# Gate, shift and scale of the first layer's modulation: native fp32 products on TensorE in four column groups, in place of sums on VectorE

## The chip, the cores and the metric

The kernel runs on one core of a Trainium2 chip, in one launch. The metric is device time in microseconds (us). Before the change it takes 1473.36 us, the median of 3 runs that lie between 1472.47 and 1473.88. Engines are named as the profile names them: PE is TensorE, DVE is VectorE, ACT is ScalarE, POOL is GpSimd, and SP is SyncE, which issues the transfers from DRAM.

## What is computed

Two transformer blocks on 256 tokens of 1024 channels. The first block has two layers, each an attention and an MLP; the second has four parallel branches and a mixture of experts. Six vectors of 1024 numbers per layer, the modulation, shift, scale and gate the data of that layer. The part of the reference that matters here is the first layer:

```python
cond = silu(c)                                   # [1, 1024]
mod = cond @ ada_w[layer] + ada_b[layer]         # [1, 6 * 1024], float32
sh1, sc1, g1, sh2, sc2, g2 = split(mod, 6)
h = rms_norm(x, norm_mix) * (1 + sc1) + sh1
x = x + g1 * even_mixer(h, ...)                  # latent and dilated attention
h = rms_norm(x, norm_mlp) * (1 + sc2) + sh2
x = x + g2 * relu(h @ w1) ** 2 @ w2
```

The change concerns `g1`, `sh2` and `sc2` of the first layer: 3072 columns of `ada_w[0]`, a product of one row of 1024 with a matrix of 1024 x 3072 (12.6 MB in float32). They are not needed before the attention's output projection is added to `x`.

## The kernel before

Tokens lie in two tiles of 128 partitions. Weights come from DRAM in units of up to 128 x 1024 floats (`unit`, `load`), each into one of four buffers named `raw`. ACT copies a unit into `hi` at reduced precision (line 318), DVE subtracts to get the rest `lo` (line 319), and in this layer POOL does every fourth subtraction instead. A product is then three PE passes over the two parts (`mm3`, lines 330 to 332) into the PSUM tiles `pj`, `ps` or `po`. Operands that are not split (attention's queries, keys, values and transposes) are multiplied as native fp32.

Layer one, `even`, runs in this order:

1. `first_columns`: the modulation's first 16 blocks of 128 columns (`sh1`, `sc1`), the normed input, and 672 columns of the projection.
2. The two latents (`latent`), normed and transposed (line 382); then two chunks of the values of the dilated heads (`dv`), two chunks of latent queries (`uq`), two of latent keys and values (`ukv`). After each chunk `fill` puts a few tiles of the modulation between (`FILL_FIRST`).
3. `weave`: the latent attention of 8 heads (`causal`, lines 635, 637, 1014), and after each head one step of the projection of the dilated queries and keys (`dilated_qk`: four chunks of four units each; `qk`, lines 552 to 606, norms and rotates them on ACT, POOL and DVE), and some tiles of the modulation (`FILL_EVEN`).
4. `dilated`: the attention of the dilated heads (lines 956 and 974), woven with the output projection and more tiles (`FILL_DIL`).
5. The rows for gate and norm are spread over the partitions (`row`, line 452), `x` is updated and normed, and the MLP starts.

A tile of the modulation is 128 columns of `ada_w`, transposed on the host, 128 x 1024: SP loads it (line 417) into one of two buffers named `ada`, and one DVE instruction (line 432, in the profile `CUSTOM_DVE_ANT_0 ada<-ada,crow`) multiplies it with the row `crow` that every partition holds and sums along the row; a short second instruction reads the sum out. Blocks 16 to 39 of 128 columns are 24 such tiles.

SP's queue is one list for all transfers. An entry waits until its buffer is free, and everything behind it waits too. What order the instructions of an engine get is made by a scheduling layer from the order in which the program writes them; `fill` asks that its tiles come on DVE behind the last subtraction. Each engine then runs its list in order.

## Time and profile before

| | |
|---|---|
| median of 3 runs | 1473.36 us |
| the profiled execution, first to last instruction | 1489.5 us |
| PE busy in it | 1376.8 us (92%) |
| DVE busy in it | 1171.3 us (79%) |
| ACT busy in it | 841.3 us (56%) |
| mean granted TensorE clock | 0.952 of full speed |
| DVE tiles of the modulation in the whole program | 132, 167.9 us |
| layer one's attention part (from the latents to the norm of the MLP) | about 52 us to 240 us |

The profiled execution is 16 us, or 1.1%, longer than the median of the runs, as profiling adds to it; steps are read from it and a result is scaled by 1473.36 / 1489.5 = 0.989. A busy PE is not a PE at its peak: the granted clock stands beside each stretch, 1.00 for 2.4 GHz and 0.50 for 1.2 GHz. A native fp32 product stands in the trace as two records of PE.

### The profile page before, as it was taken

What the parts mean: (1) busy time and instruction counts of PE and PEld (TensorE: products, weight loads), DVE (VectorE), ACT (ScalarE), POOL (GpSimd) and SP (SyncE); (2) the same over time, 40 slices, a digit from 0 to 9 for tenths busy, and PEclk for the clock granted to TensorE, in tenths of its full rate; (3) what the DMA queues carried; (4) which work ended last, traced back from release to release, by engine and by line L of the source; (5) the groups of instructions that cost most, each with busy time, mean ns of one, the idle gap of its engine ahead of it and who ended that gap; (6) DMA issues with size and microseconds to landing.
All of it is one profiled execution on the core that took longest, in us unless ns stands there. A gap on an engine that the chain in (4) does not pass through costs nothing.

```text
span 1489.5 us, 20624 instructions
## 1 busy us (share of the span) xinstructions
PE 1376.8 (92%) x7338; PEld 1140.7 (77%) x7338; DVE 1171.3 (79%) x1923; ACT 841.3 (56%) x1334; POOL 210.2 (14%) x217
## 2 busy tenths in 40 slices
PE   5778899999998989999999999999997799999996
PEld 4657678989876657988989797677785688888884
DVE  8878776787786856798775679997675898888896
ACT  4355565355544554545665556555545487777764
POOL 5557601000033301000014000000002000000001
PEclk9789899999989969999999999999999899999998
DMA  9556554889855323878744667444552599999994
GB/s 360 168 185 222 198 170 156 305 312 339 317 182 163 118 75 102 290 247 294 254 128 127 225 227 229 144 144 154 179 186 89 187 358 342 324 326 325 320 340 148
DMA packets 94414, 333.55 MB, mean 224 GB/s; under 512 B 10720, under 2 KB 11872, under 8 KB 94304
## 3 DMA queue, kind: packets, MB, share of 16 engines
q1 hardware_dynamic: 94304, 332.17, 65.5%
q8 instruction: 59, 0.97, 0.3%
q14 instruction: 51, 0.42, 0.1%
HBM read 331.08 MB, written 1.05 MB: 223 GB/s over the span
## 4 chain that ended last, share of the span: by engine, by line
PE 54%; DVE 17%; DMA 14%; issue 5%; ACT 4%; POOL 4%; SPq 0%; DVEq 0%; ACTq 0%; POOLq 0%
PE pj L330 6%; DMA raw<-in_w_dram 6%; PE pj L331 6%; PE pj L332 6%; DMA ada<-in_adaT_dram 5%; PE ps L330 5%; PE ps L332 5%; PE ps L331 5%; DVE lo L319 4%; PE ps L382 3%; DVE ada L432 3%; ACT hi L318 2%; POOL hr L471 2%; DMA raw<-in_gu_dram 2%; PE po L330 1%
## 5 line engine op out<-in xcount | busy, mean ns | idle before, releaser
L318 ACT CAST hi<-raw 128x1024 fp32r<-128x1024 f32 (+3 forms) x331 | 333.1, 1017 | 223.7 <-DMA raw<-in_w_dram 80.2
L319 DVE TENSOR_TENSOR lo<-raw,hi 128x1024 fp32r<-128x1024 f32 (+1 forms) x313 | 378.8, 1221 | 96.7 <-ACT hi L318 94.4
L432 DVE CUSTOM_DVE_ANT_0 ada<-ada,crow 128x1024 f32<-128x1024 f32 x132 | 167.9, 1280 | 32.0 <-DMA ada<-in_adaT_dram 32.0
L330 PE MATMUL pj<-hi,H 128*128 128x512 f32 (+3 forms) x392 | 154.9, 396 | 11.4 <-ACT H L734 9.0
L332 PE MATMUL pj<-hi,H 128*128 128x512 f32 (+3 forms) x392 | 151.9, 388 | 5.5 <-POOL H L737 3.4
L331 PE MATMUL pj<-lo,H 128*128 128x512 f32 (+3 forms) x392 | 151.7, 388 | 3.0 <-DVE lo L319 2.9
L1116 PE MATMUL ps<-H,lo 128*128 128x256 f32 x408 | 116.0, 284 | 2.8 <-DVE lo L319 2.7
L330 PE MATMUL pj<-hi,A 128*128 128x512 f32 (+1 forms) x293 | 115.9, 396 | 2.8 <-DVE w L879 2.0
L331 PE MATMUL pj<-lo,A 128*128 128x512 f32 (+1 forms) x293 | 115.6, 394 | 1.7 <-DVE lo L319 1.6
L1114 PE MATMUL ps<-H,hi 128*128 128x256 f32 x408 | 115.9, 284 | 0.0
L1115 PE MATMUL ps<-H,hi 128*128 128x256 f32 x408 | 115.4, 283 | 0.0
L332 PE MATMUL pj<-hi,A 128*128 128x512 f32 (+1 forms) x293 | 114.5, 391 | 0.0
L330 PEld LDWEIGHTS pj<-hi,H 128*128 128x128 f32 x392 | 76.9, 196 | 33.6 <-ACT H L734 11.6
L332 PEld LDWEIGHTS pj<-hi,H 128*128 128x128 f32 x392 | 77.3, 197 | 21.1 <-POOL H L737 6.2
L331 PEld LDWEIGHTS pj<-lo,H 128*128 128x128 f32 x392 | 77.9, 199 | 14.7 <-DVE lo L319 3.8
L1116 PEld LDWEIGHTS ps<-H,lo 128*128 128x128 f32 x408 | 78.2, 192 | 3.8 <-DVE lo L319 3.8
L1114 PEld LDWEIGHTS ps<-H,hi 128*128 128x128 f32 x408 | 78.2, 192 | 0.6 <-DVE w L543 0.2
L1115 PEld LDWEIGHTS ps<-H,hi 128*128 128x128 f32 x408 | 78.2, 192 | 0.4
L330 PE MATMUL ps<-hi,A 128*128 128x512 f32 x180 | 71.2, 396 | 0.0
L332 PE MATMUL ps<-hi,A 128*128 128x512 f32 x180 | 70.3, 391 | 0.0
L331 PE MATMUL ps<-lo,A 128*128 128x512 f32 x180 | 70.3, 390 | 0.0
L330 PEld LDWEIGHTS pj<-hi,A 128*128 128x128 f32 x293 | 55.6, 190 | 17.2 <-issue 4.4
(544 smaller groups left out, 3300.3 us busy)
## 6 DMA issues: line engine op xcount, KB each, us to landing
ada<-in_adaT_dram SPq DMA_DIRECT2D x132, 512.0 KB, 4.8
raw<-in_w_dram SPq DMA_DIRECT2D x128, 512.0 KB, 5.5
raw<-in_gu_dram SPq DMA_DIRECT2D x78, 512.0 KB, 5.9
raw<-in_in_dram SPq DMA_DIRECT2D x60, 512.0 KB, 4.6
raw<-in_down_dram SPq DMA_DIRECT2D x37, 512.0 KB, 5.6
crow<-in_gu_dram SPq DMA_DIRECT2D x34, 512.0 KB, 5.9
raw<-in_odd_in_dram SPq DMA_DIRECT2D x24, 512.0 KB, 4.8
raw<-in_even_in_dram SPq DMA_DIRECT2D x24, 384.0 KB, 3.7
```

The source lines that it names most:

```text
L318: self.nc.scalar.copy(hi, src)
L319: end = (engine or self.nc.vector).tensor_tensor(lo, src, hi, ALU.subtract)
L330: mm(ps, ah, bh, start=start, stop=False)
L331: mm(ps, ah, bl, start=False, stop=False)
L332: mm(ps, al, bh, start=False, stop=stop)
L382: self.nc.tensor.transpose(out, in_, self.ident[:p, :p])
L432: nc.vector.tensor_tensor_reduce(out=o, in0=wt, in1=r, scale=1.0, scalar=0.0, op0=ALU.mult, op1=ALU.add, accum_out=m[:, j:j + 1])
L471: nc.gpsimd.tensor_tensor(out, ss, self.mhalf[:, :ss.shape[1]], ALU.pow)
L1114: mm(ps[:, n % 2], wh, hh[:, k], start=k == 0 and n % 2 == 0, stop=False)
L1115: mm(ps[:, n % 2], wh, hl[:, k], start=False, stop=False)
L1116: mm(ps[:, n % 2], wl, hh[:, k], start=False, stop=k == 7 and n % 2 == 1)
```

## The change

The 24 DVE tiles of blocks 16 to 39 go. In their place stand three sums, one for each vector (gate, shift, scale), each of four steps. A step takes 2 x 128 rows of `ada_w[0]` and 1024 of its columns, 1 MB, laid out on the host in this order (`adaN`). Four native fp32 matmuls work on it: the column `ccol` of silu(c), repeated 32 times, is the stationary operand, 512 columns of weights the moving one, and each matmul has its own group of 32 of the array's columns, so its own 32 partitions of one PSUM tile `po`. After four steps ACT copies the sum out (`pe_end`), four small matmuls with a selection matrix turn it into columns and add the two halves of the rows, and DVE adds the bias.

The steps are no longer called by `fill` but by `steps`: 2, 2, 1, 1, 1, 1 after the six chunks of stage 2, and one after every second step of `dilated_qk`. The first eight steps are loaded into the large places `O0` and `O1` in turn, which stage 1 no longer needs and attention's output takes later; the last four into the two `ada` buffers. A step's load is issued two steps ahead of its use, once its place has been read. The stage `dilated` has none left.

```diff
+EVEN_ROOMS = ["O0", "O1"] * 4 + ["ada"] * 4
+EVEN_AHEAD = 2
+PE_EVEN = 0
-FILL_FIRST = [3, 3, 0, 0, 0, 1]
-FILL_DIL = [0, 2, 3, 0]
+FILL_FIRST = [2, 2, 1, 1, 1, 1]
-FILL_EVEN = [4, 2, 1, 2, 0, 0, 3, 2]
+FILL_EVEN = [0, 1, 0, 1, 0, 1, 0, 1]
+PE_COLS = [(512, (2048, 2560)), (512, (3072, 3584)), (512, (4096, 4608))]
...
+    def steps(self, g, n):
+        for _ in range(n):
+            next(g, None)
+
+    def with_steps(self, main, g, ns):
+        ns = iter(ns)
+        for _ in main:
+            self.steps(g, next(ns, 0))
+            yield
+        self.steps(g, 99)
...
+    def pe_load(self, parts, w):
+        n = 2 * len(parts) * w
+        for t in parts:
+            ap = bass.AP(tensor=self.A["adaN"].tensor, offset=self.pe_off, ap=[[4 * w, P], [1, t.shape[1]]])
+            self.nc.sync.dma_start(t, ap)
+            self.pe_off += t.shape[1]
+        self.pe_off += 4 * w * (P - 1)
+
+    def pe_part(self, acc, s, parts, w):
+        nc = self.nc
+        for kk in range(2):
+            t = parts[0][:, kk * 2 * w:] if len(parts) == 1 else parts[kk]
+            c = self.ccol[:, 2 * s + kk:2 * s + kk + 1].to_broadcast([P, 32])
+            for i in range(2):
+                r0 = 64 * i + 32 * kk
+                nc.tensor.matmul(acc[r0:r0 + 32, :w], c, t[:, i * w:i * w + w], start=s == 0, stop=s == 3)
+
+    def pe_even(self, at):
+        def load(s):
+            if s < len(EVEN_ROOMS):
+                r = EVEN_ROOMS[s]
+                parts = [self.T([P, D], "ada") for _ in range(2)] if r == "ada" else [self.slot(r, [P, 2 * D])]
+                self.pe_load(parts, 512)
+                tiles.append(parts)
+        tiles = []
+        for s in range(EVEN_AHEAD):
+            load(s)
+        yield
+        for s in range(len(EVEN_ROOMS)):
+            if s % 4 == 0:
+                sums = self.ps(tag="po")
+            self.pe_part(sums, s % 4, tiles[s], 512)
+            load(s + EVEN_AHEAD)
+            if s % 4 == 3:
+                j = PE_COLS[at + s // 4][1][0] // P
+                m = self.mod[0][:, j:j + 8]
+                self.nc.vector.tensor_tensor(m.rearrange("p (i j) -> p i j", i=2), self.pe_end(sums, 512),
+                                             self.cols[:, j:j + 8].rearrange("p (i j) -> p i j", i=2), ALU.add)
+            yield
+
+    def pe_end(self, acc, w):
+        nc = self.nc
+        rows = self.w()
+        nc.scalar.copy(rows[:, :w], acc[:, :w])
+        n = w // P
+        ps = self.ps()
+        for j in range(n):
+            nc.tensor.matmul(ps[:, j:j + n + 1:n], rows[:, j * P:j * P + P], self.sel, start=True, stop=True)
+        return ps[:, :2 * n].rearrange("p (i j) -> p i j", i=2)
...
-        for a, b in ((16, 24), (24, 40)):
-            self.later(0, [self.crow0], [mod], range(a, b), pool=POOL_EVEN)
+        gemv = self.pe_even(PE_EVEN)
+        next(gemv)
...
-            self.fill(FILL_FIRST[c])
+            self.steps(gemv, FILL_FIRST[c])
...
-                   dilated_qk(), FILL_EVEN, PACE_MLA)
+                   self.with_steps(dilated_qk(), gemv, FILL_EVEN), (), PACE_MLA)
...
-        self.weave(self.after_tail(dilated()), out, FILL_DIL, PACE_DIL)
+        self.weave(self.after_tail(dilated()), out, (), PACE_DIL)
```

The selection matrix adds two columns to the constants. Everything behind `dilated` is unchanged. In the order that the program gives the engines the change shows at three places; names carry buffer numbers, and line numbers of the changed kernel are its own.

SP's list at the second chunk of `dv` and the start of `uq`, before (`raw` are weights to split, `ada` tiles of the modulation):

```order
L305 DMA raw_623<-in_even_in_dram 128x768
L305 DMA raw_629<-in_even_in_dram 128x768
L417 DMA ada_620<-in_adaT_dram 128x1024
L305 DMA raw_635<-in_even_in_dram 128x768
L305 DMA raw_641<-in_even_in_dram 128x768
L417 DMA ada_699<-in_adaT_dram 128x1024
L417 DMA ada_702<-in_adaT_dram 128x1024
L305 DMA raw_708<-in_uq_dram 128x768
```

The same place after the change:

```order
L732 DMA O_139_623<-in_adaN_dram 128x2048
L732 DMA O_140_629<-in_adaN_dram 128x2048
L312 DMA raw_631<-in_even_in_dram 128x768
L312 DMA raw_637<-in_even_in_dram 128x768
L312 DMA raw_643<-in_even_in_dram 128x768
L312 DMA raw_649<-in_even_in_dram 128x768
L732 DMA O_155_711<-in_adaN_dram 128x2048
L732 DMA O_156_717<-in_adaN_dram 128x2048
L312 DMA raw_727<-in_uq_dram 128x768
```

Two loads of 1 MB now stand ahead of the four units of a chunk, where single tiles of half a MB stood between them.

PE's list between `first_columns` and the first chunk of `dv`, before (`ps` from `w` are the latents' transposes):

```order
L382 MATMUL ps_472<-consts_67,w_470 128x128 x3
L382 MATMUL ps_494<-consts_67,w_484 128x128 x2
L330 MATMUL pj_562<-hi_540,H_31_145 128x384
L330 MATMUL pj_563<-hi_540,H_31_145 128x384
L331 MATMUL pj_562<-lo_541,H_31_145 128x384
```

The same place after:

```order
L401 MATMUL ps_472<-consts_67,w_470 128x128 x3
L401 MATMUL ps_494<-consts_67,w_484 128x128 x2
L744 MATMUL po_618<-O_120_536,ccol_65 32x512
L401 MATMUL ps_507<-consts_67,w_505 128x128 x3
L401 MATMUL ps_529<-consts_67,w_519 128x128 x2
L744 MATMUL po_618<-O_120_536,ccol_65 32x512 x3
L744 MATMUL po_618<-O_121_538,ccol_65 32x512 x4
L337 MATMUL pj_566<-hi_544,H_31_145 128x384
```

The first two steps, eight matmuls, and the transposes of the second tile of tokens moved ahead of the first chunk's products. Steps three and four stand in the same way between the two chunks of `dv`, five and six between `dv` and `uq`, and the others among later work.

DVE's list in the weave, around the third and fourth chunk of `dilated_qk`, before:

```order
L319 TENSOR_TENSOR lo_1495<-raw_1492,hi_1494 128x768
L1025 RECIPROCAL sm_1461<-sm_1461 128x2
L606 TENSOR_TENSOR w_1385<-w_1385,hr_1394 128x384
L623 TENSOR_SCALAR sc_1463<-sc_1463,sm_1461 128x128
L432 ISA ada_1555,mod_1_61<-ada_1555,crow_75 128x1024
L432 ISA mod_1_61 128x1
L432 ISA ada_1558,mod_1_61<-ada_1558,crow_75 128x1024
L432 ISA mod_1_61 128x1
L606 TENSOR_TENSOR w_1435<-w_1435,hr_1444 128x384
```

The like place after:

```order
L625 TENSOR_TENSOR w_1477<-w_1477,hr_1486 128x384
L1101 RECIPROCAL sm_1507<-sm_1507 128x2
L642 TENSOR_SCALAR sc_1509<-sc_1509,sm_1507 128x128
L326 TENSOR_TENSOR lo_1936<-raw_1933,hi_1935 128x1024
L593 TENSOR_TENSOR w_1588<-pj_1544,tabk_1350 128x384
```

The tiles of line 432 that stood between attention's and the projection's short instructions are gone, and nothing takes their place on DVE but one addition of 128 x 8 for each of the three sums.

## Rows read from the trace of the kernel before

**Rows 1.** Busy time by stretch: length, PE, PEld, DVE, ACT, POOL; clock, DMA share, GB/s.

```profile
63.00:84.00 21.00, 19.66 (x109) 18.38 (x107) 16.88 (x30) 8.71 (x18) 7.08 (x6) 1.00 0.72 238
84.00:108.00 24.00, 16.39 (x73) 12.05 (x74) 17.84 (x42) 14.06 (x33) 20.04 (x30) 0.85 0.45 154
108.00:150.00 42.00, 35.98 (x188) 32.91 (x187) 37.19 (x79) 21.71 (x51) 26.96 (x24) 0.91 0.68 219
150.00:180.00 30.00, 25.00 (x127) 20.79 (x126) 25.24 (x49) 17.25 (x39) 24.83 (x22) 0.90 0.61 203
180.00:196.00 16.00, 16.00 (x59) 10.53 (x58) 9.80 (x30) 5.99 (x15) 0.00 (x0) 0.60 0.31 102
```

**Rows 2.** The same view of line 432 alone, DVE only; the sum is 52 to 240.

```profile
108.00:150.00 42.00, 14.12 (x18) 0.91 0.68 219
150.00:180.00 30.00, 8.29 (x11) 0.90 0.61 203
...
sum 188.00, DVE 37.08; mean DVE 4.63
```

**Rows 3.** Chain of waits, 64 to 85 us: start, length, engine and line.

```profile
64.56 2.37 DVE ada L432
...
67.82 4.96 DMA raw<-in_even_in_dram
...
72.88 0.84 ACT hi L318
...
75.64 8.02 issue
```

**Rows 4.** SP's list in order of time, 39 to 110 us.

```profile
66.97 0.33 SPq L417 DMA_DIRECT2D ada<-in_adaT_dram  x1
...
72.52 0.84 SPq L305 DMA_DIRECT2D raw<-in_uq_dram  x2
```

**Rows 5.** Busy time in 10 us stretches, the fastest transfers of the layer (columns of rows 1).

```profile
20.00:30.00 10.00, 6.42 (x29) 5.20 (x29) 9.72 (x17) 2.49 (x4) 8.14 (x5) 0.95 1.03 402
```

**Rows 6.** Chain of waits in the weave: pieces of DVE's tiles.

```profile
143.95 2.78 DVE ada L432
...
158.88 1.07 DVE ada L432
...
160.03 3.35 DVE ada L432
```

**Rows 7.** The same chain: long pieces of POOL.

```profile
121.54 2.06 POOL w L575
...
129.40 2.18 POOL hr L471
...
166.41 2.08 POOL w L575
...
172.56 1.93 POOL w L575
```

**Rows 8.** Lines 575 and 471, 52 to 180 us: ns shortest/median/longest, first and last start.

```profile
L575 POOL TENSOR_TENSOR w<-w,xn x12: 451/998/2082, 85.8 to 172.6; 128x384 f32<-128x384 f32 x8, 128x128 f32<-128x128 f32 x4
...
L471 POOL TENSOR_TENSOR hr<-hr,mhalf x16: 1007/1336/2184, 87.6 to 174.9; 128x4 f32<-128x4 f32 x8, 128x6 f32<-128x6 f32 x8
```

**Rows 9.** PE in order of time: native fp32 in two groups of 64 columns, line 956.

```profile
210.14 0.38 PE L956 MATMUL po<-pt,row 128*64 128x256 f32 x1
210.15 0.38 PE L956 MATMUL po<-sc,row 128*64 128x256 f32 x1
...
210.37 0.38 PE L956 MATMUL po<-sc,row 128*64 128x256 f32 x1
...
211.66 0.38 PE L956 MATMUL po<-es,crow 128*64 128x128 f32 x2
211.97 0.50 PE L330 MATMUL po<-hi,O 128*128 128x512 f32 x1
```

**Rows 10.** Weight loads of the transposes, 50 to 225 us: busy us, mean ns.

```profile
L382 PEld LDWEIGHTS ps<-consts,w 128*128 128x128 f32 x34 | 4.9, 166 | 7.3 <-issue 3.7 <-DVE w L606 1.8 <-DVE w L849 0.9
```

More of the change, by code (lines that the diff above doesn't have):

```diff
@@ L56 @@
 GATE = [((2,2),(1,1)), ((),()), ((2,2),(1,1)), ((),())]
-FILL_FIRST = [3, 3, 0, 0, 0, 1]
-FILL_DIL = [0, 2, 3, 0]
-POOL_EVEN = ()
+EVEN_ROOMS = ["O0", "O1"] * 4 + ["ada"] * 4
+EVEN_AHEAD = 2
+PE_EVEN = 0
+FILL_FIRST = [2, 2, 1, 1, 1, 1]
 PT = 1
@@ L130, in constants @@
         np.broadcast_to(invf(), (P, 48)),
+        (np.arange(P)[:, None] % 32 == 0) & (np.arange(P)[:, None] // 64 == np.arange(2)[None, :]),
         masks.reshape(P, 1024),
@@ L139, in constants @@
     return np.concatenate([np.asarray(x, np.float32) for x in parts], 1)
-CONST_W = 128 + 1024 + 128 + 128 + 128 + 16 + 1 + 16 + 48
+CONST_W = 128 + 1024 + 128 + 128 + 128 + 16 + 1 + 16 + 48 + 2
 def invf():
@@ L193, in lay_out @@
     r["even_in"] = pack(a["even_w_in"][0], even_units())
+    r["adaN"] = np.concatenate([
+        np.stack([a["ada_w"][0][:, c:c + w].reshape(4, 2, P, w).transpose(0, 2, 1, 3) for c in cs], 3).reshape(-1)
+        for w, cs in PE_COLS])
     r["uq"] = pack(a["mla_w_uq"][0].reshape(384, 768), units(384, [(0, 384), (384, 768)]))
@@ L657, in setup @@
         c = self.T([P, CONST_W - 768], "consts")
-        nc.sync.dma_start(c[:, :176], A["consts"][:, :176])
+        nc.sync.dma_start(c[:, :178], A["consts"][:, :178])
         pi = self.T([P, 2], "posi", dt=I32)
@@ L666, in setup @@
         self.crow0 = self.row(col, "crow")
+        self.ccol = col
         inv = c[:, 128:176]
-        self.mask = c[:, 176:432]
-        self.utri = c[:, 432:560]
-        self.iota = c[:, 560:688]
-        ax = c[:, 688:816].rearrange("p (t c f) -> p t c f", t=2, c=2)
+        self.sel = c[:, 176:178]
+        self.mask = c[:, 178:434]
+        self.utri = c[:, 434:562]
+        self.iota = c[:, 562:690]
+        ax = c[:, 690:818].rearrange("p (t c f) -> p t c f", t=2, c=2)
         self.acos, self.asin = ax[:, :, 0], ax[:, :, 1]
-        self.rank16 = c[:, 816:832]
-        self.pidx = c[:, 832:833]
-        self.halves = c[:, 833:849]
+        self.rank16 = c[:, 818:834]
+        self.pidx = c[:, 834:835]
+        self.halves = c[:, 835:851]
+        self.pe_at = self.pe_off = 0
         self.mhalf = self.T([P, 8], "mhalf")
@@ L693, in setup @@
         next(latents)
-        nc.sync.dma_start(c[:, 176:432], A["consts"][:, 176:432])
-        nc.sync.dma_start(c[:, 432:], A["consts"][:, 1200:])
+        nc.sync.dma_start(c[:, 178:434], A["consts"][:, 178:434])
+        nc.sync.dma_start(c[:, 434:], A["consts"][:, 1202:])
         self.gains = self.slot("A5", [P, NGAIN1])
@@ L698, in setup @@
         self.va = self.slot("A4", [P, 2048])
-        nc.sync.dma_start(self.va[:, 1024:1792], A["consts"][:, 432:1200])
+        nc.sync.dma_start(self.va[:, 1024:1792], A["consts"][:, 434:1202])
         self.dmasks = self.va[:, 1024:1792].rearrange("p (m k) -> p m k", m=3)
@@ L910, in even @@
             self.proj(st, D, acts, f)
-            self.fill(FILL_FIRST[c])
+            self.steps(gemv, FILL_FIRST[c])
         for c in range(2):
             self.proj(su, 384, [(cq[:, 0], cq[:, 1], 0), (cq[:, 0], cq[:, 1], P)], q_evac(c))
-            self.fill(FILL_FIRST[2 + c])
+            self.steps(gemv, FILL_FIRST[2 + c])
         sk = Stream(A["ukv"], units(256, COLS_1024))
@@ L917, in even @@
             self.proj(sk, 256, [(ck[:, 0], ck[:, 1], 0), (ck[:, 0], ck[:, 1], P)], kv_evac(c))
-            self.fill(FILL_FIRST[4 + c])
+            self.steps(gemv, FILL_FIRST[4 + c])
         self.flush()
```

## The prediction

> **What bounds the kernel now.** I read the busy times by stretch first, then the chain of waits through the same stretches, then the lists of the engines that the chain names. Only 52 to 240 us matters: nothing behind it is edited. The busy times [rows 1] show four different limits. From 63 to 84 us PE is the limit: busy 19.66 of 21 us at full clock, on the two chunks of `dv`. From 84 to 108 it is the short work on queries and keys, with POOL at 20.04 of 24 us. From 108 to 180, the weave, DVE has the most to do: 37.19 + 25.24 = 62.4 of 72 us, beside PE's 61.0 and POOL's 51.8. From 180 to 196 PE is busy for all 16 us, with a mean clock of 0.60. DVE's tiles of the modulation take 37.1 us of the whole [rows 2], 14.1 of them from 108 to 150 alone; but only where the chain runs through them are they time. It does so four times: once at 64.56, for 2.37 us [rows 3], and three times in the weave, for 2.78, 1.07 and 3.35 us [rows 6]. After 164 us no tile is on the chain, so the five tiles taken from `dilated` are worth nothing directly.
>
> **The change, part by part.**
>
> *The tile at 64.56.* It ends at 66.93, and with it an `ada` buffer comes free; SP issues the next tile at 66.97 and only then the two units of weights queued behind it, the last of which lands 4.96 us after 67.82 [rows 3, 4]. From 75.64 to 83.66 PE streams products [rows 3]. The 2.37 us go, but the same place in SP's list now holds something else. Two loads of 1 MB wait until steps 1 and 2 have read their places, and all four units of the second chunk (1.6 MB) wait behind them. Steps 1 and 2 stand on PE behind the latents' transposes, so I put their end at 62 to 64 us. The fastest transfers of this layer move 402 GB/s [rows 5]: 3.7 MB then take 9.2 us, and the last unit lands at 72 to 73, where it lands today. Nothing is won there. Between the chunks PE must do steps 3 and 4, and behind the second chunk steps 5 and 6, in a stretch where it is the limit. `uq`, asked for at 72.52 today [rows 4], is now asked for behind two further loads that wait for step 4, at about 75, and lands 8 us later. By hand along these rows the first products of `uq` end near 87 us, where the chain has `uq`'s first rotation at 83.7 today, right behind the 8.02 us of products [rows 3]. **Term 1: +4.0 us**, between 0 (PE's steps fall into gaps) and +8 (each of the three pairs of loads holds up what follows).
>
> *What a step costs on PE.* No row shows four groups of 32 columns. The nearest row is line 956, native fp32 in two groups of 64: records of both groups start 0.01 us apart, and the next one of the same group follows 0.22 us later for 256 columns [rows 9]. So two groups run side by side at no extra cost, and 512 columns take 0.43 us a record, 0.86 us for the two records of a matmul. If four groups run like two, a step costs 0.86 us and the 12 steps 10.3; two by two 20.6; one at a time 41.3. I take the first, as nothing in the row shows one group slowing the other. Six of the twelve lie in or before the PE-bound stretch and are in term 1. Of the others three lie in 84 to 108 us, where PE is idle 7.6 us [rows 1], and three in the weave, where it is idle 11 of 72. The three ends of sums add 12 small matmuls, each with two loads of 128 columns at 0.17 us [rows 10], 4.1 us in all, and an ACT copy each, of 512 columns, below the 0.84 us of a `hi` of 768 [rows 3], on an engine that is half idle. Of these 2.6 + 4.1 us I count a fifth to a quarter on the chain, the share in which PE has no gap near. **Term 2: +1.5 us**, between 0 and +5 (half clock, or two by two).
>
> One rule speaks against the change. At the end of line 956's work the next record would start 0.11 us after the one at 211.77 (the second of the pair at 211.66), but line 330 starts at 211.97 [rows 9]: about 0.1 us is lost when PE goes from two groups back to the whole array. The Trainium skill, TensorEngine Tiling (Array Packing), Key Properties, says that changing the tiling mode drains the engine; the trace agrees, at 0.1 us. With some 12 visits of two changes each that is 2.4 us of PE, about 0.8 of it on the chain: the sum would be 0.8 us worse.
>
> *The weave.* The three tiles on the chain go: 2.78 + 1.07 + 3.35 = **term 3: -7.2 us**. What is late next? After the first comes a `lo` subtraction on DVE that waited for its turn alone, so it moves up in full. After the other two come the factor of a head's norm and two short instructions whose inputs were ready; POOL would be next, and is in line. It may take back half, so the term lies between -3.6 and -7.2.
>
> *POOL beside DVE.* Equal instructions of POOL differ widely: line 575 takes 451 to 2082 ns, median 998; line 471 1007 to 2184, median 1336 [rows 8]. The long ones stand on the chain, at 121.54, 129.40, 166.41 and 172.56 [rows 7], and DVE's tiles, which read two tensors from SBUF, run at those times, themselves up to 3.35 us [rows 6]. Against the medians the four are 1.1 + 0.8 + 1.1 + 0.9 = 3.9 us too long, and one subtraction on POOL about 0.7 more. But DVE's other instructions will move into the places of the tiles. **Term 4: -2.8 us**, between 0 and -6. The Trainium skill, GPSIMD Engine Reference, Specifications, names this contention: the engine shares its SBUF interfaces with VectorE, in conflict with instructions that have two SBUF inputs. By it `lo` subtractions would stretch POOL as the tiles do, and term 4 would be nearer to -1.5.
>
> *`dilated` and the rest.* Its tiles lay beside a PE that is busy all the time [rows 1]: 0. The half clock there, a mean of 0.60 while PE is busy 16.00 of 16 us, could fall elsewhere once the work ahead has moved: between -3 and +3. The constants' two further columns cost nothing that a row shows.
>
> **Sum:** 4.0 + 1.5 - 7.2 - 2.8 = -4.5 us, 1489.5 to 1485.0 us in the profiled execution; times 0.989, 1468.9 us for the median, 0.3% faster.
>
> **The rivals.**
>
> *The weave opens up (1462 us).* With the tiles' 14.1 + 8.3 = 22.4 us gone from DVE's 62.4 [rows 2], 40 of 72 us, the three engines' queues untangle: weights are asked for earlier, since SP no longer waits for tiles there, term 4 is -6, and term 1 stays near 1. The sum is 1.0 + 1.0 - 7.2 - 6.0 = -11.2, so 1478.3 in the profiled execution and a median near 1462. For it: DVE is the busiest engine of the stretch. Against it: PE with 61.0 and POOL with 51.8 of 72 us leave little room [rows 1].
>
> *SP's list and PE's steps lock each other (1479 us).* One mechanism: a load of a step waits for a step on PE, the units of weights wait behind that load, and the products behind the next steps wait for those units. It happens three times, at the second chunk of `dv`, at `uq` and at `ukv`. It decides the sign from the point at which a unit lands after PE has come to it: for `uq` I expect 2 us late, and if each place costs 4 to 5 us, term 1 is +13 and half of terms 3 and 4 (-5.0) does not make up for it with term 2 at 1.5: +9.5 in the worst case, +6 as its middle, a median of 1479. For it: every step in the first stage sits in a stretch where PE is the limit [rows 1]. Against it: DVE's tiles hold SP's list in the same manner today [rows 4].
>
> *The groups run two by two (1473.5 us).* Then the six early steps cost 5.2 us more, of which 4 are on the chain, and the late ones 0.6: -4.5 + 4.6 = 0. Against it: two groups of 64 do not slow each other [rows 9]. One group at a time would be +15 or so; the row excludes that for two groups.
>
> The Trainium skill, TensorE: Matmul & The Clock Gate, Measured speedup vs the span model, gives 2.38 times for three column tiles, not 3. Four at the same efficiency would be 3.2 times, an estimate from that page: a step of 1.1 us, which would put the sum near -3.3. No run here shows it yet.
>
> That the change does not do what it says has no chance worth a number: the tiles are gone from DVE's list.
>
> **How the numbers follow.** The forecast -4.5 us has 0.40, with its own range of -8.5 to -1, 1465 to 1472.5. The weave opens: 0.20. Two by two, or gain and cost cancel: 0.13. The lock: 0.27. A measurement here tells 0.2%, 2.9 us, from no change: faster is below 1470.4, slower above 1476.3. Of the forecast's 0.40 about 0.30 lies below 1470.4 and 0.10 within; the second adds 0.20 faster; the third 0.08 same, 0.03 slower and 0.02 faster; the lock 0.04 same, 0.23 slower. Faster 0.52, same 0.22, slower 0.26. The range that leaves out 2 in 10 reaches from a weave that opens a little further than above, 1458, to the lock's upper half, 1480.
>
> **What would show it.** In the changed profile, 108 to 180 us should shrink by 8 to 10 us, with DVE busy about 40 us there and no piece of 2 to 3 us of DVE on the chain. Line 575's median should fall. Four matmuls of line 744 should start within 0.05 us, and a step last 0.9 us at full clock. `uq`'s products should come 3 to 4 us later. I am wrong if the first stage does not get longer, if four groups do not overlap, or if the weave is no shorter in spite of a free DVE: then POOL or PE had been the limit there.

## The result, and the profile after

The changed kernel takes 1503.88 us, the median of 4 runs between 1496.45 and 1511.20, beside 1473.62 of the kernel before on the same chip: a ratio of 1.0149, 95% interval 1.0105 to 1.0193. By the ratio it is slower by some 22 us; the two medians alone lie 30 us apart, which is more than that interval allows, and the four runs of the kernel before spread from 1472.47 to 1484.41. Either way it is slower, where 0.3% faster was forecast, and the median lies outside the range. Its profiled execution has a span of 1500.3 us.

Two more times put the forecast's base right. A second trace of the kernel before, taken with the experiments, has a span of 1480.7 us, and its timed runs there lie between 1470.10 and 1490.09. So the 1489.5 us that I had scaled by 0.989 were a long execution, not a longer one because of the profiler. Its first layer is no different: the mark at the end of the attention part that is used below stands at 214.7 us in the first trace and at 213.5 in the second.

First the busy times of the changed kernel by stretch: length, PE, PEld, DVE, ACT, POOL with records in brackets, granted clock, DMA share, GB/s. They answer to [rows 1]; 196 to 212 is added.

```profile
63.00:84.00 21.00, 20.84 (x124) 16.53 (x117) 6.85 (x15) 7.24 (x12) 5.39 (x2) 0.94 0.83 315
84.00:108.00 24.00, 21.12 (x108) 12.95 (x107) 11.51 (x28) 9.50 (x20) 10.63 (x21) 0.93 0.61 224
108.00:150.00 42.00, 31.71 (x184) 26.33 (x182) 28.77 (x65) 26.02 (x62) 27.51 (x29) 0.97 0.50 154
150.00:180.00 30.00, 28.45 (x162) 23.83 (x162) 18.13 (x46) 17.21 (x41) 17.42 (x19) 0.93 0.56 194
...
196.00:212.00 16.00, 16.00 (x52) 10.80 (x52) 7.38 (x28) 7.50 (x15) 0.00 (x0) 0.50 0.00 0
```

DVE has become idle: 46.9 of the 72 us from 108 to 180, where it had 62.4. Nothing got shorter for it. From 84 to 108 us PE has 21.12 us to do where it had 16.39, and from 196 to 212 it runs at half clock throughout.

Equal stretches hide that all stages have moved, so from here I read by marks of the program: the first score of the weave, the first score of the dilated heads, and the first product of the output projection's last part, which starts beside the spreading of the gate's row (the row mark). The expectations call this third mark the MLP, which it is not: the MLP's own first product comes at 227.47 us before and at 244.90 after, 12.8 and 12.9 us behind it. Between 52 us and these three marks the views of the kernel before (its first trace), then of the changed one, have these rows (columns as above).

```profile
52.00:108.60 56.60, 45.23 (x212) 38.17 (x213) 42.34 (x99) 28.78 (x67) 31.75 (x47) 0.86 0.57 187
108.60:180.40 71.80, 60.77 (x312) 53.20 (x311) 62.24 (x122) 39.29 (x89) 51.79 (x45) 0.90 0.64 212
180.40:214.70 34.30, 34.30 (x186) 24.52 (x185) 23.88 (x74) 20.74 (x39) 2.39 (x1) 0.82 0.48 155
```

```profile
52.00:120.60 68.60, 59.11 (x310) 41.30 (x311) 33.08 (x87) 29.45 (x68) 29.27 (x47) 0.93 0.60 221
120.60:192.20 71.60, 59.52 (x327) 49.54 (x325) 45.37 (x111) 39.01 (x91) 41.42 (x44) 0.90 0.52 166
192.20:232.00 39.80, 39.80 (x194) 29.04 (x193) 17.82 (x49) 21.76 (x40) 3.64 (x2) 0.75 0.24 79
```

So the first stage takes 12.0 us more (forecast: some 4 to 5), the weave 0.2 less (forecast: 8 to 10 less), the dilated stage 5.5 more (forecast: 0). At the row mark the changed kernel is 17.3 us behind, at the MLP's own first product 17.4. What lies behind that mark takes 1268.3 us, and 1274.8 and 1267.2 in the two traces of before: nothing that the change reaches.

Where the first stage's 12 us arise, the chain of waits of the changed kernel shows (start, length, engine and line; lines 337 to 339 are products, 744 the steps, 778 the small matmuls of a sum's end, 732 the steps' loads).

```profile
61.85 0.42 PE ps L401 x2
62.27 3.48 PE po L744 x14
65.75 0.55 PE pj L337 x2
...
74.27 1.90 PE po L744 x16
...
76.83 1.05 PE ps L778 x8
...
85.97 1.04 PE po L744 x8
87.03 0.33 SPq L732
87.42 0.42 issue
87.84 4.93 DMA raw<-in_uq_dram
```

The work that was to fit between other work is the chain itself. Of the first stage's 68.6 us the steps hold 10.8% of the chain and the ends 3.1%, together 9.5 us. The first product of `dv` starts at 65.68; before it was 58.88. PE's own list shows why, before first, then after (start, length, line, in brackets the idle time ahead and what ended it).

```profile
58.88 0.62 PE L330 MATMUL pj<-hi,H 128*128 128x384 f32 x2 [1.34 <-ACT hi L318]
```

```profile
57.40 1.04 PE L744 MATMUL po<-O,ccol 128*32 128x512 f32 x2
61.08 0.52 PE L401 MATMUL ps<-consts,w 128*128 128x128 f32 x3 [2.63 <-DVE w L925]
61.85 0.42 PE L401 MATMUL ps<-consts,w 128*128 128x128 f32 x2 [0.26 <-DVE w L925]
62.20 3.55 PE L744 MATMUL po<-O,ccol 128*32 128x512 f32 x14
65.68 0.62 PE L337 MATMUL pj<-hi,H 128*128 128x384 f32 x2
```

Before, `dv`'s products ran in the gaps of the second latents. Now they stand behind the transposes of those latents and behind fourteen of the first two steps' sixteen records. `uq`'s first product comes at 87.76 in place of 78.75, and its last unit of weights waits until 87.03 for step 5 and lands at 92.77. So of the 12.0 us, 6.8 are there when `dv` starts, 9.0 when `uq` starts, and the last 3.0 come between `uq` and the weave.

At full clock the steps are as fast as was hoped: the two of 74.27 are 16 records in 1.90 us, 0.95 us a step. The first two take more than twice as long: 1.04 us for two of their records, and 3.55 for the other fourteen, at a granted clock of 0.52 (62.2 to 65.7 us).

What the waits on SyncE's list do here can be read in part from the same trace. First the loads' waits for steps in SyncE's queue from 52 to 120.6 us (total, times, longest), then PE from the first product of `dv` to `uq`'s last unit (length, PE, clock, DMA share, GB/s).

```profile
SPq L732 <- PE po L744: 38.4, 6, 12.7
```

```profile
65.70:92.90 27.20, 27.04 (x166) 1.00 0.80 305
```

SyncE waits long, but PE has work all the time up to 92.9 us. Only then does it lose 0.44 and 1.82 us at `uq`'s last unit.

### The profile page after: what moved, and what is told of

It is laid out like the page before. It is cut to its first block, busy times and chain, and to the rows that moved or that the text cites. A ratio compares the mean times of both kernels' runs of the same rounds, so it can differ in the third digit from the quotient of the medians.

```text
span 1500.3 us, 20830 instructions
## 1 busy us (share of the span) xinstructions
PE 1395.3 (93%) x7458; PEld 1144.5 (76%) x7458; DVE 1140.4 (76%) x1876; ACT 842.9 (56%) x1337; POOL 199.9 (13%) x217
## 3 DMA queue, kind: packets, MB, share of 16 engines
HBM read 331.08 MB, written 1.05 MB: 221 GB/s over the span
## 4 chain that ended last, share of the span: by engine, by line
PE 57%; DVE 17%; DMA 12%; issue 5%; ACT 5%; POOL 4%; SPq 0%; DVEq 0%; ACTq 0%; POOLq 0%
PE pj L337 7%; PE pj L339 6%; PE pj L338 6%; DMA raw<-in_w_dram 5%; DMA ada<-in_adaT_dram 5%; PE ps L337 5%; PE ps L339 5%; PE ps L338 5%; DVE lo L326 4%; PE ps L401 3%; DVE ada L451 2%; ACT hi L325 2%; POOL hr L490 2%; PE ps L1192 2%; PE ps L1190 2%
## 5 line engine op out<-in xcount | busy, mean ns | idle before, releaser
L451 DVE CUSTOM_DVE_ANT_0 ada<-ada,crow 128x1024 f32<-128x1024 f32 x108 | 130.9, 1221 | 25.5 <-DMA ada<-in_adaT_dram 25.1
L338 PE MATMUL pj<-lo,A 128*128 128x512 f32 (+1 forms) x293 | 115.2, 393 | 3.6 <-POOL lo L326 1.8
L338 PEld LDWEIGHTS pj<-lo,A 128*128 128x128 f32 x293 | 55.2, 188 | 16.4 <-DVE lo L326 2.7
```

The lines of the kernel that those rows point to most:

```text
L338: mm(ps, ah, bl, start=False, stop=False)
L451: nc.vector.tensor_tensor_reduce(out=o, in0=wt, in1=r, scale=1.0, scalar=0.0, op0=ALU.mult, op1=ALU.add, accum_out=m[:, j:j + 1])
```

## The experiments

Where a kernel's modulation is not the reference's, the second block loads its experts' weights as the data fall (151 transfers of `gu` in place of 78 in the first experiment, whose whole takes 1792 us). Of these kernels only the first layer is read. A kernel that leaves something out also gets another order from the scheduling layer; differences between kernels are differences of whole schedules. Each variant was traced once.

### Neither form of the work: e1_none

```diff
-                parts = [self.T([P, D], "ada") for _ in range(2)] if r == "ada" else [self.slot(r, [P, 2 * D])]
-                self.pe_load(parts, 512)
-                tiles.append(parts)
+                pass
...
-            if s % 4 == 0:
-                sums = self.ps(tag="po")
-            self.pe_part(sums, s % 4, tiles[s], 512)
...
-                self.nc.vector.tensor_tensor(m.rearrange("p (i j) -> p i j", i=2), self.pe_end(sums, 512),
-                                             self.cols[:, j:j + 8].rearrange("p (i j) -> p i j", i=2), ALU.add)
+                self.nc.vector.tensor_copy(m, self.cols[:, j:j + 8])
```

> The changed kernel with neither the 12 steps on TensorE nor their loads: the gate, shift and scale of the first layer are left out (bias alone). What is left is layer one without either form of the work. Theory A (my sum's weave term falls: DVE's tiles were not what the weave waits for; it is a chain of short instructions across ACT, POOL and DVE in fixed lists): the weave, from the first score product to the first score of the dilated heads, still takes 70 to 73 us (71.8 before, 71.6 after), the first stage ends at 106 to 109 us, and the whole lands at 1462 to 1472 us. Theory B (the forecast's terms 3 and 4 were right and the steps in the weave ate them up): the weave takes 61 to 65 us here, the whole 1454 to 1462 us.

```profile
52.00:104.20 52.20, 41.43 (x216) 36.40 (x216) 33.19 (x83) 29.99 (x68) 29.68 (x47) 0.93 0.48 153
104.20:170.90 66.70, 57.26 (x306) 50.50 (x304) 45.26 (x110) 37.58 (x87) 41.44 (x44) 0.90 0.39 125
170.90:200.90 30.00, 30.00 (x190) 22.13 (x189) 16.94 (x48) 21.43 (x41) 3.67 (x2) 1.00 0.29 103
```

Between the two theories. Without the tiles the first stage is 4.4 us shorter than before, the weave 5.1, the dilated stage 4.3, of which 3.8 in the scores, which run at full clock here. The gain of 9.5 us up to the dilated heads is close to the forecast's 10.0 for terms 3 and 4, though half of it lies in the first stage. The gain was there; the steps with their loads took it, and more: from this kernel to the changed one it is 16.4 us up to the weave, 21.3 up to the dilated heads and 31.1 up to the row mark.

### Loads without steps, steps without loads: e2_loads, e3_steps

```diff
-            if s % 4 == 0:
-                sums = self.ps(tag="po")
-            self.pe_part(sums, s % 4, tiles[s], 512)
...
+                self.nc.vector.tensor_copy(m, self.cols[:, j:j + 8])
```

> The changed kernel with all its loads of the steps but without their matmuls (gate, shift and scale are left out, bias alone): no transfer waits for a step on TensorE. Theory A (the first stage's 12 us come from the steps' places in TensorE's list): the weave starts at 106 to 110 us, as before. Theory B (they come from 8 MB of loads ahead of the units of weights in SyncE's list): it starts at 114 to 118 us. If both take part, 111 to 113.

```diff
-            if s < len(EVEN_ROOMS):
+            if s in (0, 1, 8):
...
-            self.pe_part(sums, s % 4, tiles[s], 512)
+            self.pe_part(sums, s % 4, tiles[s % 2 if s < 8 else 2], 512)
```

> The changed kernel with all 12 steps on TensorE, but only three of their twelve loads: the steps read the same places again, so the sums are not the modulation's, and no unit of weights waits behind a load that waits for a step. Theory A (TensorE's list): the weave still starts at 117 to 120 us. Theory B (SyncE's list): it starts at 108 to 112 us, 3 to 4 us of it for the steps' own time on TensorE.

With the loads alone the weave starts at 126.0 us, later than with both: without steps to wait for, the loads come at other times. Its mean clock up to there is 0.78, beside 0.93 in the changed kernel. That result lies outside both theories and does not tell the causes apart. With the steps alone the rows are:

```profile
52.00:112.90 60.90, 53.35 (x298) 40.03 (x298) 34.07 (x86) 31.39 (x70) 29.74 (x47) 0.95 0.43 133
112.90:185.50 72.60, 61.72 (x338) 51.21 (x336) 46.36 (x111) 38.11 (x89) 40.13 (x44) 0.90 0.41 129
185.50:225.10 39.60, 39.60 (x194) 28.82 (x193) 17.82 (x49) 21.76 (x40) 3.64 (x2) 0.75 0.24 80
```

112.9 lies between the theories. Against the kernel without the work the steps cost 8.7 us in the first stage, 5.9 in the weave and 9.6 in the dilated stage, where the clock is 0.75 in place of 1.00. The changed kernel, with all its loads, is another 7.7 us later at the weave. From 214.7 us the way to 232.0 is thus -13.8 for the tiles, +24.2 for the steps, +6.9 for the loads, if the steps are added first. With the loads first, by e2_loads (dilated heads at 194.4, row mark at 224.4), it is -13.8, +23.5 for the loads, +7.6 for the steps; up to the weave the steps would then even save 5.4. Only the sum of the two, 31.1 us, does not hang on the order in which they are added.

### The loads' size: e6_bytes

```diff
-            ap = bass.AP(tensor=self.A["adaN"].tensor, offset=self.pe_off, ap=[[4 * w, P], [1, t.shape[1]]])
-            self.nc.sync.dma_start(t, ap)
+            ap = bass.AP(tensor=self.A["adaN"].tensor, offset=self.pe_off, ap=[[4 * w, P], [1, w]])
+            self.nc.sync.dma_start(t[:, :w], ap)
...
-                nc.tensor.matmul(acc[r0:r0 + 32, :w], c, t[:, i * w:i * w + w], start=s == 0, stop=s == 3)
+                nc.tensor.matmul(acc[r0:r0 + 32, :w], c, t[:, :w], start=s == 0, stop=s == 3)
```

> The changed kernel with the same loads in the same places of SyncE's list, but 256 KB for each step in place of 1 MB (all four matmuls of a step read the same 512 columns, so the sums are not the modulation's). The changed kernel starts its weave at 120.6 us, with the loads left out it was 112.9. Theory A (the bytes: 8 MB more in the first stage): it starts at 112 to 115 us. Theory B (the lock: a load waits for a step and the units of weights wait behind it, whatever its size): 118 to 121 us.

```profile
52.00:115.20 63.20, 53.92 (x300) 42.35 (x301) 37.37 (x92) 31.64 (x71) 29.93 (x47) 0.91 0.51 155
```

The weave starts at 115.2 us, 5.4 earlier than in the changed kernel, nearly as theory A said. But the places did not stay: `dv`'s first product stands at 60.44 us, in the gaps again, and SyncE's waits for steps fall from 38.4 us to this:

```profile
SPq L732 <- PE po L744: 8.8, 4, 7.0
```

The bytes and the waits went together, so the run does not separate them; what the lock cost beyond PE's idle time at `uq` stays open.

### The order on TensorE: e4_behind, e12_full

```diff
     def steps(self, g, n):
         for _ in range(n):
-            next(g, None)
+            with self.tc.issue_after(self.product.ins):
+                next(g, None)
...
-        mm(ps, al, bh, start=False, stop=stop)
+        self.product = mm(ps, al, bh, start=False, stop=stop)
```

> The changed kernel with one more rule for the order: a step's matmuls stand on TensorE behind the last product written ahead of them, so the first two no longer stand ahead of the first chunk of values, behind the second latents' transposes. The loads move back in SyncE's list with them. Theory A: the first chunk's products fill TensorE's gaps beside the latents again, the weave starts at 109 to 113 us in place of 120.6, and the whole is 8 to 12 us under the changed kernel's. Theory B (SyncE's list or the mere work on TensorE): it starts at 117 us or later.

My theory fell: 120.3 us for the weave's start, 191.9 for the dilated heads, as without the rule, and 1496.41 us (ratio to before 1.0114, 1.0051 to 1.0177). The edit did not do what it was to do: `dv`'s first product comes at 62.38 us in place of 65.68, but still behind all the latents' transposes and not in their gaps, and later PE waits 4.58 us, up to 111.99, for a subtraction on DVE. So the run does not test whether the gaps are worth the difference. The same rule on the kernel with three loads shows whether the loads are behind it:

> The kernel of e3_steps (all steps, three of twelve loads, so the sums are not the modulation's) with the rule of e4_behind: the same TensorE time of the steps at other places, the first two behind the first chunk of values and the rest after later products, with no load for them to wait for. e3_steps reached the weave at 112.9 us and the dilated heads at 185.5, the kernel without the work at 104.2 and 170.9. Theory A (the steps cost their own 14.6 us of TensorE wherever they stand): dilated heads at 184 to 188. Theory B (what they cost is set by the place): under 181 or over 190.

It also comes to the weave at 120.8 and to the dilated heads at 191.9, 21.0 us behind the kernel without the work, where e3_steps was 14.6 behind with the same steps. Theory B holds: the same steps cost more in another order, and the loads are not needed for it. The start of `dv` alone does not decide when the weave starts: in e3_steps it comes at 67.14 us, later than in the changed kernel, and the weave 7.7 us earlier. A part of the difference can be the clock: its mean in the first stage is 0.85 in e12_full and 0.95 in e3_steps. An estimate of the time that a lowered clock can cost, 0.15 of 68.8 us less 0.05 of 60.9, is 10.3 - 3.0 = 7.3 us at most, beside a difference of 7.9; but the two traces of the kernel before, at 0.86 and 0.93, differ by only 0.7 us there. No run separates the order from the clock that comes with it. Behind the weave e12_full makes up for it: its dilated stage runs at 0.99 and takes 30.6 us, so it reaches the row mark at 222.5, ahead of e3_steps at 225.1.

One of the places, in PE's list of e12_full just ahead of the weave:

```profile
115.84 1.05 PE L779 MATMUL ps<-consts,w 128*128 128x2 f32 x8 [2.48 <-ACT w L775]
116.76 1.56 PE L402 MATMUL ps<-consts,w 128*96 128x128 f32 x8
...
119.18 1.74 PE L402 MATMUL ps<-consts,w 128*96 128x128 f32 x8 [0.54 <-DVE mod L767]
120.75 0.82 PE L655 MATMUL ps<-A,A 96*128 96x128 f32 x4
```

The end of the second sum stands ahead of the last transposes of queries and keys (line 402). It waits 2.48 us for ACT's copy of the sum, then takes 1.05, and the transposes and the first scores (line 655) queue behind it. In the changed kernel the same end stands there too, with a wait of 0.85 us and 1.05 of its own up to 118.55. Four matmuls of two columns in eight records, which I had costed at 0.17 us a weight load, some 1.4 us, are 1.9 us there and 3.5 in e12_full.

### Half as much TensorE time: e5_half

```diff
-                nc.tensor.matmul(acc[r0:r0 + 32, :w], c, t[:, i * w:i * w + w], start=s == 0, stop=s == 3)
+                nc.tensor.matmul(acc[r0:r0 + 32, :w // 2], c, t[:, i * w:i * w + w // 2], start=s == 0, stop=s == 3)
...
-        nc.scalar.copy(rows[:, :w], acc[:, :w])
+        nc.scalar.copy(rows[:, :w // 2], acc[:, :w // 2])
+        nc.scalar.copy(rows[:, w // 2:w], acc[:, :w // 2])
```

> The kernel of e3_steps (steps on TensorE with three of twelve loads) with each of the steps' matmuls half as wide, 256 columns, so the steps take some 5.7 us of TensorE in place of 11.5; number, places and waits are unchanged, and the sums are not the modulation's. The kernel without the work came to the first score of the dilated heads at 170.9 us, the one with the steps at 185.5, 14.6 us later. Theory A (what costs is TensorE's own time: none of it is hidden): 178 to 181 us. Theory B (what costs is the places in TensorE's list, where products behind a step wait with it): 183 to 187 us.

The dilated heads start at 181.0, as theory A said, but the run does not tell the theories apart: the places did change. Line 744 alone, in three stretches of this kernel (length, PE, PEld, clock, DMA share, GB/s):

```profile
52.00:90.00 38.00, 5.65 (x58) 2.23 (x58) 0.86 0.52 164
90.00:112.00 22.00, 2.77 (x38) 0.98 (x38) 0.92 0.43 135
112.00:181.00 69.00, 0.00 (x0) 0.00 (x0) 0.89 0.40 123
```

All twelve steps have left the weave, where e3_steps, with full width, has four.

### Later steps, later tiles: e11_late, e10_tiles

```diff
-EVEN_ROOMS = ["O0", "O1"] * 4 + ["ada"] * 4
+EVEN_ROOMS = ["O0", "O1"] + ["ada"] * 10
-FILL_FIRST = [2, 2, 1, 1, 1, 1]
+FILL_FIRST = [0, 0, 0, 0, 1, 1]
-FILL_EVEN = [0, 1, 0, 1, 0, 1, 0, 1]
+FILL_EVEN = [2, 1, 1, 1, 1, 1, 2, 1]
```

> The changed kernel with ten of the twelve steps in the weave, two at the end of the first stage, and the rule of e4_behind; only the first two steps are loaded into the large places, so the first stage carries 2 MB of the work in place of 8. Theory A (the 8 MB cost the first stage some 7 us, the steps cost TensorE's own time of 14 us wherever they stand): the weave starts at 107 to 110 us and takes 76 to 81, so the dilated heads start at 184 to 190 us in place of 192.2, still behind the 180.4 of before; the whole is 3 to 8 us less than the changed kernel's. Theory B (the weave has room for the steps): the weave takes 68 to 72 us and the dilated heads start at 175 to 180.

```profile
52.00:112.10 60.10, 44.06 (x227) 37.13 (x226) 34.05 (x85) 30.39 (x68) 29.45 (x47) 0.87 0.42 135
112.10:197.80 85.70, 79.11 (x417) 54.94 (x416) 43.75 (x111) 40.94 (x91) 41.56 (x45) 0.96 0.64 218
```

Worse than theory A: the weave takes 85.7 us, 19.0 more than without the work, and the dilated heads start at 197.8. The weave has no room for ten steps. The dilated stage then runs at full clock, so that the MLP's own first product comes at 239.25 us, 5.7 ahead of the changed kernel's; the whole is still slower than before (1488.54 to 1512.67 us in four runs, ratio 1.0174, 1.0120 to 1.0228). Moving the kernel before's own tiles is no way out either:

```diff
-FILL_FIRST = [3, 3, 0, 0, 0, 1]
-FILL_DIL = [0, 2, 3, 0]
+FILL_FIRST = [3, 0, 0, 0, 0, 0]
+FILL_DIL = [2, 4, 4, 4]
-FILL_EVEN = [4, 2, 1, 2, 0, 0, 3, 2]
+FILL_EVEN = [2, 1, 1, 1, 1, 1, 0, 0]
```

> The kernel before with its 24 tiles on VectorE kept but moved: 14 of them stand beside the dilated heads in place of five, 7 in the weave in place of 14, three in the first stage in place of seven (the lists of numbers are all that changes). Without any of this work the weave took 66.7 us and the first stage ended at 104.2. Theory A (the tiles cost time in the weave and the first stage, and nothing beside the dilated heads, where TensorE is busy throughout): first stage 105 to 107, weave 67 to 70, the whole 3 to 8 us less than before. Theory B (VectorE's or SyncE's list gives it back in the dilated stage, where twice as many tiles and 7 MB stand in 32 us): the dilated stage grows by 4 us or more, and the whole is within 3 us of before.

The first stage ends at 107.2 as said, but the weave takes 76.1 us and the stretch up to the row mark 40.6, at a clock of 0.73 (1497.27 us, ratio 1.0127, 1.0091 to 1.0163). The dilated stage grows as theory B said; the whole, some 18 us more, fits neither. Nor did the tiles move as planned: 25 records of line 432, two for a tile, still stand in the weave (16.99 us), where the kernel before has 29 (22.81 us). So the weave is 4.3 us longer with somewhat less work of the tiles in it: their busy time alone does not set its length.

### The clock of the dilated stage: e7_warm, e8_warm

```diff
-        mm(ps, al, bh, start=False, stop=stop)
+        self.product = mm(ps, al, bh, start=False, stop=stop)
+
+    def warm(self, n):
+        ps, h = self.ps(tag="pj"), self.h[0]
+        with self.tc.issue_after(self.product.ins):
+            for _ in range(n):
+                self.nc.tensor.matmul(ps, h[:, 0, :P], h[:, 0:2], start=True, stop=True)
...
+        self.warm(24)
         self.weave(self.after_tail(dilated()), out, (), PACE_DIL)
```

> The changed kernel with 24 products of 128 x 512 that nobody reads, placed on TensorE behind the last product of the dilated queries and keys, where it otherwise waits for the last heads; nothing else is changed. In the changed kernel the clock is granted at half from 184 to 212 us, over the whole of the dilated scores, which take 24.1 us; without the modulation's work it was at full, and they took 15.4. Theory A (the clock falls in the idle time ahead of the stage, and the stage's own work does not bring it back): the clock stays at 1.00 from the end of the weave, the scores take 15 to 17 us, and the whole is 6 to 10 us under the changed kernel's. Theory B (the stage's own work or what the steps left behind holds the clock down): the scores take 22 us or more, and the whole is not less.

> The kernel before with the same 24 unread products at the same place. Its clock is at half from 180 to 193 us of the dilated scores, which take 19.2 us. Theory A of e7_warm: the scores take 15 to 17 us, and the whole is 3 to 7 us less than before, so 1467 to 1475 us beside 1478. Theory B: no gain, or 1 to 3 us more.

The changed kernel first, then the one with 24 unread products; both around the start of the dilated scores (192.2 and 197.3 us).

```profile
184.00:188.00 4.00, 3.23 (x15) 3.19 (x16) 2.89 (x8) 0.85 (x3) 2.08 (x3) 0.62 0.89 294
188.00:192.00 4.00, 3.58 (x14) 1.76 (x12) 1.41 (x6) 1.12 (x3) 0.37 (x1) 0.50 0.66 235
192.00:204.00 12.00, 12.00 (x43) 8.20 (x41) 4.85 (x15) 4.09 (x10) 0.00 (x0) 0.50 0.00 0
204.00:212.00 8.00, 8.00 (x23) 5.71 (x23) 3.92 (x17) 4.67 (x9) 0.00 (x0) 0.50 0.00 0
212.00:220.00 8.00, 8.00 (x48) 5.70 (x49) 4.33 (x11) 5.85 (x11) 2.37 (x1) 0.98 0.27 72
```

```profile
190.00:194.00 4.00, 4.00 (x14) 2.56 (x13) 0.72 (x4) 0.85 (x2) 0.00 (x0) 0.50 0.30 123
194.00:197.00 3.00, 3.00 (x11) 2.30 (x11) 0.00 (x0) 0.00 (x0) 0.00 (x0) 0.66 0.00 0
197.00:205.00 8.00, 8.00 (x50) 5.70 (x49) 5.23 (x20) 4.13 (x10) 0.00 (x0) 1.00 0.00 0
```

The scores come out nearly as theory A said, the time does not. With the products the clock is up by 197 us and the scores take 14.8 us in place of 24.1. But most of the products ran at half clock themselves, the dilated heads start 5.1 us later, and the row mark is at 231.6, as without them (232.0). The whole is no better: 1504.16 us, ratio 1.0160, 1.0114 to 1.0206. Nor is it so that the stage's own work never brings the clock back: it rises within the stage at 212 us in the changed kernel and at 192 in the kernel before. In the kernel before the same insert takes the scores from 19.2 to 16.3 us and the row mark to 209.1, 4.4 to 5.6 us earlier than in its two traces; yet the whole is the same (1481.51 us, ratio 1.0015, 0.9989 to 1.0041). Where these us go behind the mark is not shown. In no run did a clock of 1.00 that was brought about in this way make the whole shorter.

### The kernel before again: e9_before

> The kernel before, unchanged: a second trace of it beside those of the variants. The first one, which the forecast used, reaches the first score of the weave at 108.6 us, that of the dilated heads at 180.4, and the MLP at 214.7, and its 1489.5 us are at the slow end of this kernel's runs (1470 to 1490). If the stages of the first layer vary from run to run, the MLP starts at 205 to 211 us here; if what varies lies behind them, within 2 us of 214.7.

213.5 us at the row mark, within 2 us of the first trace: in these two traces the first layer is steady, and what varies lies behind it. The differences of 4 to 24 us above are read against this 1.2, which is one repeat of one kernel.

## Why the prediction was wrong

**Term 1 is the step that failed.** I put it at +4.0 us between 0 and 8; the first stage took 12.0 more, although leaving the tiles out gives 4.4 back there: steps and loads cost it 16.4 (e1_none against the changed kernel). I had followed the weights of `dv` ("Nothing is won there") and put at nothing the delay of its products. The order that I showed had PE's first steps and the second latents' transposes ahead of `dv`, and the stretch of 63 to 84 us was named as PE's limit, but the gaps in which `dv` ran before 63 us (they lie ahead of [rows 3]) were not read. In the changed kernel `dv` starts 6.8 us late, behind fourteen records of the first two steps that take 3.55 us at a clock of 0.52. Steps 3 to 6 and the first end then add 1.9, 1.9 and 1.05 on a PE that has no idle time; `dv` itself takes some 2.6 us less, in part by the clock, which before was 0.60 from 60 to 64 us. So `uq` starts 9.0 us late where I said 3 to 4. That is how the 12.0 us arise in this order. How much of them another order would save is not shown, since every variant moved other things too; nor is what the loads cost by bytes and by waits.

**Term 2 had the right price and the wrong share.** A step takes 0.95 us at full clock where I said 0.86 to 0.9. The sum had a slip: 2.6 us is three of the six later steps; all six and the ends would be 5.2 + 4.1, and a fifth to a quarter of that 1.9 to 2.3 us, not enough to matter. The 0.1 us that a change of tiling was to cost is in this trace too: the step at 74.20 follows the product at 73.94 by 0.26 us, where products follow one another by 0.17. But the share itself was a guess from PE's idle time, 7.6 and 11 us. The steps' cost up to the dilated heads is 14.6 us in e3_steps, as much as twelve steps and three ends at 0.95 and 1.05 (11.4 + 3.2), and 21.0 in e12_full, more than all of it; after the loads alone it is nothing (192.2 beside 194.4 us). That the first of these equals the full price is thus no rule. The reading that fits: idle time in a list that runs in order is time in which PE waits for something; a step that stands ahead of the awaited work delays what follows, and an end of a sum adds a wait of its own.

**Terms 3 and 4 were nearly right as a gain and wrong as a result.** Taking the tiles away gave 9.5 us up to the dilated heads, against 10.0. That these agree is luck: both terms were for the weave, and the weave gave 5.1. In the changed weave nothing of it is left: with three steps and one end in it (3.9 us at 0.95 and 1.05) it takes 71.6 us against 66.7. POOL's long instructions did shrink: line 471, now 490, is at most 1337 ns where it was 2184, and line 575, now 594, at most 1741 where it was 2082, but its median stayed (1004 ns, [rows 8]).

```profile
L594 POOL TENSOR_TENSOR w<-w,xn x12: 453/1004/1741, 91.4 to 183.9; 128x384 f32<-128x384 f32 x8, 128x128 f32<-128x128 f32 x4
...
L490 POOL TENSOR_TENSOR hr<-hr,mhalf x16: 1007/1190/1337, 93.2 to 187.0; 128x4 f32<-128x4 f32 x8, 128x6 f32<-128x6 f32 x8
```

In the changed weave DVE, with little else in its list, waits for POOL, and PE for DVE. From the changed kernel's lists of DVE and of PE:

```profile
140.03 0.94 DVE L625 TENSOR_TENSOR w<-w,hr 128x384 f32<-128x384 f32 x1 [3.94 <-POOL hr L490]
```

```profile
150.13 0.69 PE L1090 MATMUL po<-es,A 128*64 128x256 f32 x1 [5.01 <-DVE es L634]
```

My reading is that the tiles filled such waits before, so that the weave gained little from fewer of DVE's 62.4 us. It is a reading only: e1_none has the same kind of waits, and its weave is 5.1 us shorter.

**The dilated stage was not 0.** Its bound of 3 us was too narrow: it took 5.5 us more, with the clock at 0.50 for the first 20 us of it. The kernel before has it at 0.50 for some 12 us, from 180.4 to 192 ([rows 1] show the mean of 0.60); that this could grow by 8 us they did not show. What decides when it rises stays open: e12_full also comes to the stage at 0.50, and there it is at full from 192.9 us on, a us after the first score.

**The rivals.** The lock had the right sign, with a chance of 0.27, and its term of +13 is near the first stage's 12.0. But its 4 to 5 us a place were for products that wait for late units, and the changed kernel's PE has no such idle time at the second chunk of `dv` and 2.3 us at `uq`; what the waits cost otherwise was not separated from the loads' bytes. The delay of `dv`'s products behind the steps on PE, and a dilated stage that is 5.5 us longer at a lower clock, were in no rival. The groups two by two are excluded by the 0.95 us. The weave that opens up is excluded for this order, and e1_none's 66.7 us show how far it could open: 5 us.

**What stays open.** Why the weave takes 66.7, 72.6, 76.1 or 85.7 us is read as the order of the lists, but no run holds the order fixed and changes a duration, and the clock changes with the order. No version here beats the kernel before: TensorE's time for these 3072 columns was at no tried place cheaper than VectorE's.

## What to carry to other kernels

Idle time of an engine that runs its list in order is not room by itself: before work is put there, find the instruction that the engine waits for and ask what stands behind the new work. Price a moved step at its full time plus the wait of its own end unless a row shows the gap it fits in, and read the gaps in which the displaced work ran, not only the transfers that feed it. Where half of the gain is to come from a freed engine, take the work out altogether in one run first: it costs one kernel and gives the ceiling. And look at the order that a variant really got before reading it as a test: here at least four of them (e4_behind, e5_half, e6_bytes, e10_tiles) moved other things than they were meant to.

## What the hardware showed

Four column groups of 32 run side by side in native fp32: one after the other the four matmuls of a step would take 3.4 us, an estimate from line 956's 0.86 [rows 9], and a step took 0.95 at a clock of 1.00, 3.6 times less. The Trainium skill, TensorE: Matmul & The Clock Gate, Measured speedup vs the span model, gives 2.38 for three column tiles. Here the measurement is better than the 3.2 that the prediction estimated from it for four.

The changed kernel's dilated stage shows the granted clock at 0.50 for 20 us in which PE is busy all the time. The Trainium skill, TensorE: Matmul & The Clock Gate, Part 1: The HAM clock gate, has a busy engine at full clock; here the measurement differs, with 0.50 in a stretch in which the profile has PE busy 12.00 of 12 us, and it decides. e1_none, e2_loads and e11_late, which enter the stage at full clock, keep it (up to the row mark the stage is 30.0 us at a clock of 1.00 in e1_none, beside 34.3 at 0.82 before the change and 39.8 at 0.75 after it). Entering it at 0.50 does not settle the matter, as e12_full shows just ahead of its dilated scores and from the first of them on:

```profile
188.00:191.90 3.90, 3.08 (x12) 1.77 (x12) 1.49 (x7) 0.85 (x2) 0.08 (x1) 0.50 0.62 210
191.90:206.80 14.90, 14.90 (x84) 11.32 (x84) 8.88 (x33) 10.91 (x22) 0.83 (x1) 0.99 0.00 0
```

In e7_warm the clock rose in the stretch that ended the 24 products of 128 x 512.
